# A two-layer decoder trunk on one core: new load order at the start, a reordered sequence of weight pairs, another attention pace, and a split last block

## The chip, the cores and the metric

The kernel runs on one NeuronCore of a Trainium2 chip. The metric is the device time of one execution in microseconds, the median of several runs. One execution of each kernel is also recorded by the hardware profiler; its trace is what the rows below come from.

## What is computed

One inference step of a trunk of two layers over 1024 prompt positions and 8 sample rows (1032 columns in the kernel's layout), width 1024, all in float32. The reference of a layer, shortened:

```
xa, za, u, v, zb, q, k, vv, zc, gates = split(x @ w_in)      # 5632 columns
ya = pool_mix(xa)                    # causal windows 2/4/8/16, mean minus x, 64x64 mix
yb = u * spatial(layer_norm(v))      # 128-position chunks, lower-triangular weights
yc = window_attention(rope(q), rope(k), vv, sinks)           # window 128, 8 heads, 2 kv heads
g  = sigmoid(gates + b_gate)         # 3 x 1024
merged = g0*((ya*silu(za)) @ w_pa) + g1*((yb*silu(zb)) @ w_pb) + g2*((yc*silu(zc)) @ w_pc)
x  = layer_norm(ALPHA*x + merged @ w_out)
```

Beside the two results the step returns the pooling state, the key and value caches and the normalised v rows.

## The kernel before

**Arithmetic.** Every float32 operand is split into a rounded part h and a remainder lo (`split`, L96: ACT writes h, VectorE writes lo), and a product is three matmuls, h by h, h by lo and lo by h. x lies transposed in XH and XL, 8 tiles of 128 rows by 1032 columns.

**Stages of a layer.** (1) `a0` (L348) computes v and the input of its norm for nine row blocks with the eight weight slices w0 (wA); block b needs x block b, split by `split_x`. Its normalisation (`a0_post`) reads the rows lrow. (2) `rope` (L382) makes keys and queries, with weights wB. (3) Eighteen *pairs* (`pair`, L870): each computes two column tiles of w_in with seven products of 24 matmuls (a Strassen scheme: `product`, quarters of x and sums of quarters T2, T3, T4), and evacuates partial sums with VectorE adds (L878) and a `use` function of the pair: `gates` (12 pairs: tanh on ACT into two tiles, stored to DRAM by ACT's queue), `pair_xa` (the input of the pooling), `pair_z` (two: silu2 of za, zb), `pair_u`, `gate_c` (two: silu of zc times the attention's output). (4) `project` (L980): 24 steps (branch i, tile d); a step multiplies a branch output by its weights, and VectorE (L1000) multiplies with the gate read back from DRAM. (5) the output projection `d_mm` in two column halves, then `d_ln`, `d_out`, for nine row blocks in the order 0, 1, 2, 8, 3, 4, 5, 6, 7.

**What sets the order.** It is written out by hand; each engine runs its instructions in program order. Small work is put between matmuls by `Jobs` (L29): each call of `pump` is a tick; a pair has 21 (two in each product, L866, and seven in `pair`). List 1 is the attention; a step of it that uses TensorE blocks the list for `pace` ticks (L343). `need(key)` runs whatever is still open up to that key. Weights come by `Feed` (L80): SP issues a load when a raw buffer (six tiles "wr") is free; `prep` splits one; four split weights ("wh") fit. GpSimd makes the weight sums that a pair needs (L210 to L219), and the sums of the pooling (L770, L775), which VectorE finishes (`pool_widen` L795, `pool_mean` L805); `pool_mix` (L818) follows on TensorE. Big tiles are named by slots (x0 to x11, u4 to u11): a tile waits until the slot's previous user is done. All DMAs share a small set of semaphores used in turn, so an issue also waits until an earlier DMA on its semaphore has landed.

**Loads at the start.** SP issues x0's first half, wA0, wA1, x0's second half, wA2 to wA5, x1; ACT issues x3, x5, x7 (L1103); SP goes on with wA6, wA7, ident, x2, lrow, x4, x6, the sample rows, lcol, cb, then six tiles of wB.

Of the kernel before, what the change touches and what calls it, by code (L numbers as in the profile page):

```python
# [8 lines left out]
F32 = mybir.dt.float32  # L9
F32R = mybir.dt.float32r  # L10
AF = mybir.ActivationFunctionType
ALU = mybir.AluOpType
# [4 lines left out]
L = 2  # L17
# [5 lines left out]
DM = 1024  # L23
SEGS = ((0, 384), (384, 384), (768, 264))
ALPHA = 4.0 ** 0.25
EPS = 1e-5


# [51 lines left out]
class Feed:  # L80
# [2 lines left out]
    def __init__(self, nc, new, items):  # L83
        self.nc, self.new, self.items, self.raw = nc, new, deque(items), deque()

    def stage(self, n=1):
        for _ in range(n):
            if self.items:
                src = self.items.popleft()
                c = src.free_size()  # L90
                t = self.new()[:, 0:c]
                self.nc.sync.dma_start(out=t, in_=src)
                self.raw.append(t)

# [7 lines left out]
def trunk_kernel(  # L102
# [23 lines left out]
    def t_acc():  # L126
        return acc.tile([128, 512], F32, tag="acc", name="acc")
# [16 lines left out]
    def t_sm(n, name, bufs=4):  # L144
        return sm.tile([128, n], F32, tag=name, name=name, bufs=bufs)

    def t_u(s, shape, dt=F32, name="u"):

        return big.tile([128] + shape, dt, tag=s, name=f"{name}{s}")
# [16 lines left out]
    def blk(b):  # L166
        return slice(b * 128, b * 128 + 128) if b < NB else slice(S, T)
# [4 lines left out]
    def order():  # L172
        for l in range(L):
            yield from [wA[l, :, k] for k in range(8)]
            yield from [wB[l, j, :, 4 * h:4 * h + 4] for j in range(5) for h in range(2)]
            yield from [wS[l, p, q] for p in range(18) for q in range(4)]
            yield from [wP[l, d, :, h * 512:h * 512 + 512] for h in range(2) for d in range(2)]
            for d in range(2, 8):
                yield from [wP[l, d, :, h * 512:h * 512 + 512] for h in range(2)]
                if d >= 4:  # L180
                    yield wO[l, 0, :, d - 4]
            yield from [wO[l, 0, :, k] for k in range(4, 8)]
            yield from [wO[l, 1, :, k] for k in range(8)]
# [12 lines left out]
    def prep(n=1):  # L196
        for _ in range(n):
            if todo:
                todo.popleft()()
# [45 lines left out]
    class Slices:  # L245
# [2 lines left out]
        def __init__(self, slots, cols=512):  # L248
            self.h, self.lo, self.slots, self.cols = {}, {}, slots, cols

        def prep(self, n=1):
            for _ in range(n):
                k, c = len(self.h), self.cols
                if k < 8:
                    if len(self.slots) == 4 and k == 0:
                        self.p = t_p(name="slp")
                    t = self.p[:, k] if len(self.slots) == 4 and k < 4 else t_u(self.slots[k % len(self.slots)], [T], F32R, "sl")
                    self.h[k], self.lo[k] = t[:, 0:c], t[:, 512:512 + c]
                    split(nc, self.h[k], self.lo[k], feed.raw.popleft())
                    feed.stage()  # L260

    ident = const.tile([128, 128], F32, name="ident")
    cb = const.tile([128, 428], F32, name="cb")
# [74 lines left out]
    class Layer:  # L338
        def __init__(self, l):
            self.l, self.c, self.jobs = l, LC[l], Jobs()  # L340
            self.s, self.pt, self.res, self.rr, self.row, self.y = [{} for _ in range(6)]
            self.late, self.step, self.out = deque(), 0, []
            self.jobs.pace = 2.8  # L343
            self.kT = t_u("u10", [T], F32, "kT")
            self.v = t_u("u11", [NB, 128], F32, "v")
            self.vs = lay.tile([NS, 128], F32, name="vs")
# [573 lines left out]
            out(0, 1)  # L920
            pump()

        def gates(self, i, d, extra={}):
            O = [t_u(s, [T], F32, "g") for s in (("u8", "u9") if d % 4 else ("u6", "u7"))]

            def use(c, q, s, p):
                o = O[c][:, q * HT + s * 258:q * HT + s * 258 + 258]
                A.activation(o, p, AF.Tanh, bias=self.c["h"][:, i * 8 + d + c:i * 8 + d + c + 1], scale=0.5)  # L928
                if s and (c, q) in ((1, 0), (0, 1)):
                    A.dma_start(out=gd[i][d + c], in_=O[c])  # L930

            self.pair(use, O, extra)

        def gate_c(self, j, extra={}):
            O = [t_u(s, [T], F32, "z") for s in (("u6", "u7") if j else ("u4", "u5"))]

            def use(c, q, s, p):
                e = slice(q * HT + s * 258, q * HT + s * 258 + 258)
                t, o, y = t_w2()[:, 0:258], O[c][:, e], self.ycr[:, j + c, e]
                A.activation(t, p, AF.Tanh, scale=0.5)  # L940
                V.scalar_tensor_tensor(o, t, 1.0, p, op0=ALU.add, op1=ALU.mult)
                V.scalar_tensor_tensor(y, o, 0.5, y, op0=ALU.mult, op1=ALU.mult)

            self.pair(use, O, extra)

        def split_y(self, j, eng=None):
            h, lo = [t_u(f"x{4 + 2 * j + i}", [T], F32R, "yh") for i in range(2)]
# [32 lines left out]
        def project(self):  # L980
            for x, (i, d) in enumerate(self.steps):
# [5 lines left out]
                for q in range(2):  # L987
# [21 lines left out]
                        self.late.append((self.step + 1, lambda d=d, q=q, m=m[:, e]: self.merged(d, q, m)))  # L1009
                    if (i < 2 and q) or (i == 2 and not q and d >= 3):  # L1010
                        prep()
                if x < 3:
                    self.split_c((1, 3, 2)[x])
                if x == 0:
                    for q in range(2):
                        self.load_gate(0, 1, q)
# [16 lines left out]
        def d_mm(self, b, h, w):  # L1033
            n = rows(b)
            x = self.res.pop((b, h))
            p = mm_rows(b, w, self.jobs)
            if h == 0:
                if b < NB:
                    t = t_u(("u11", "u10", "u4", "u5", "x0", "x1", "x2", "x3")[b], [T], F32, "rr")
                    self.row[b] = [t[:, 0:512], t[:, 512:1024]]  # L1040
                else:
                    self.row[b] = [whp.tile([128, 512], F32, tag="wh", name="rs") for _ in range(2)]
                self.rr[b] = t_sm(16, "rr", 9)
            r = self.row[b][h]
            V.scalar_tensor_tensor(r[:n], x[:n, 0:512], 2 * ALPHA, p[:n], op0=ALU.mult, op1=ALU.add)  # L1045
            V.bn_stats(self.rr[b][:n, h * 6:h * 6 + 6], r[:n])  # L1046

        def d_ln(self, b):
            n, c = rows(b), self.c
            rw = self.row[b]  # L1050
            st, mv = self.rr[b][:, 0:12], self.rr[b][:, 12:14]
            V.bn_aggr(mv[:n], st[:n])  # L1052
            rstd_of(mv, n, 4 * EPS)
            g, be = c["lng"], c["lnb"]
            if self.l == L - 1 and b == NB - 1:
                for h in range(2):
                    r = rw[h]
                    V.scalar_tensor_tensor(r, r, mv[:, 0:1], g[h], op0=ALU.subtract, op1=ALU.mult)  # L1058
                for h in range(2):
                    r = rw[h]  # L1060
                    V.scalar_tensor_tensor(r, r, mv[:, 1:2], be[h], op0=ALU.mult, op1=ALU.add)  # L1061
                return
            for h in range(2):
                r = rw[h][:n]
                V.tensor_scalar(r, r, mv[:n, 0:1], mv[:n, 1:2], op0=ALU.subtract, op1=ALU.mult)
            for h in range(2):
                r = rw[h][:n]
                V.tensor_tensor(r, r, g[h][:n], op=ALU.mult)
                G.tensor_tensor(r, r, be[h][:n], op=ALU.add)
# [29 lines left out]
    def load_x(b, ks=slice(0, 8)):  # L1099
        if b not in xraw:  # L1100
            t = t_u(f"x{b if b < 4 else b + 4}" if b < NB else "u8", [T], F32, "x")
            xraw[b] = t[:, 0:8 * rows(b)].rearrange("p (k t) -> p k t", k=8)
        (A if b in (3, 5, 7) else SP).dma_start(out=xraw[b][:, ks], in_=xb[b][:, ks] if b < NB else xs[:, ks])  # L1103

    def split_x(b, ks=slice(0, 8)):
        split(nc, XH[:, ks, blk(b)], XL[:, ks, blk(b)], xraw[b][:, ks])
        if b == NB:
            stack_sample()
# [6 lines left out]
    feed.stage(2)  # L1115
    load_x(0, hi_k)
    feed.stage(4)
    load_x(1, lo_k)
    load_x(1, hi_k)
    w0 = Slices(WA, 384)  # L1120
    split_x(0, lo_k)
    w0.prep(2)
    SP.dma_start(out=ident, in_=c_a)
    for b in range(2, NB + 1):
        load_x(b)
        if b == 2:
            load_rows(0)
    load_layer(0)
    SP.dma_start(out=cb, in_=c_b)
    V.memset(mhalf, -0.5)  # L1130
    V.memset(XS.bitcast(F32), 0.0)
    split_x(0, hi_k)
    w0.prep(6)

    order_d = [0, 1, 2, 8, 3, 4, 5, 6, 7]
    left = []
    for l in range(L):
# [35 lines left out]
                J.need(("TT", n, k))  # L1173
        y.t1_parts()
        y.queue_sample()
        for i in range(3):
            for d in range(0, 8, 2):
                if (i, d) == (0, 2):
                    J.need("sp")
                y.gates(i, d, {3: lambda: J.need(("T1", 3))} if (i, d) == (0, 0) else {})  # L1180
        J.need(("P", NB - 1, 1))
        y.pair_xa()
        y.ya = y.pair_z(("u8", "u9"))
        y.queue_mix()
        J.need(("pool", 1))
# [3 lines left out]
        y.pair_u()  # L1189
        J.need(("sgu", 1))  # L1190
        y.gate_c(0)
        y.open_gates()
        for i, d in ((0, 0), (1, 0)):
            for q in range(2):
                y.load_gate(i, d, q)
        y.gate_c(2, {2: lambda: y.split_y(0), 21: lambda: y.split_y(1), 3: lambda: y.split_y(2),
                     1: lambda: y.split_y(3), 4: lambda: y.split_c(0)})
        for q in range(2):
            y.load_gate(1, 1, q)
        cur["w0"] = w0 = Slices(WA)  # L1200
# [140 lines left out]
```

## Time and profile before

| | |
|---|---|
| median of 3 runs | 1469.99 us (1469.11 to 1471.54) |
| profiled execution | 1468.98 us, its span 1467.2 us |
| TensorE matmuls | 1436.6 us busy, 98% of the span |
| VectorE, ACT, GpSimd busy | 70%, 41%, 30% |
| mean granted TensorE clock | 0.999 |
| layer 0 | first blocks from 4.89 us, pairs 107.6 to 540.0, projection from 540.0 |
| last matmul starts, span ends | 1459.15, 1467.2 us |

How to read it: TensorE is busy almost throughout, so the profile is read for the moments in which it isn't: the waits of TensorE with the instruction that ended them. Windows give the busy time of each engine between two moments; here they are cut at the pair boundaries.

### The profile page before, as it was taken

The numbers are of one execution on the slowest core, as the hardware profiler recorded it, in microseconds if no ns is written. First come the engines' busy times: TensorE is split into PE (matmuls) and PEld (weight loads), VectorE is DVE, ScalarE is ACT, GpSimd is POOL, SyncE is SP. The second block draws the span as 40 slices with busy tenths as digits, with TensorE's granted clock in tenths as the row PEclk, the third lists the DMA queues.
The fourth block names the chain that finished last, engine by engine and source line by source line (L and its number), as shares of the span: only waits on it lengthen the run. The fifth ranks groups of instructions, "written<-read, shape, count | busy, mean of one in ns | idle before, by whom it ended". The sixth has DMA issues, their size and how long they took to land. (4 is left out here: it accounts for less than half of the span.)

```text
span 1467.2 us, 27711 instructions
## 1 busy us (share of the span) xinstructions
PE 1436.6 (98%) x10592; PEld 1356.2 (92%) x10592; DVE 1030.5 (70%) x2330; ACT 603.3 (41%) x1419; POOL 438.7 (30%) x434
## 2 busy tenths in 40 slices
PE   7999999999999999999999999999999999999997
PEld 7999999999998999988799999999999999999876
DVE  6997676676558687654889966666665777966547
ACT  4375565556533252220224745555565232422100
POOL 0114334141242205500530251423321522054015
PEclk9999999999999999999999999999999999999999
DMA  6312222323223135643324122222222231466413
GB/s 253 125 46 80 87 94 66 102 73 102 73 84 76 44 102 188 204 142 94 134 93 139 53 73 96 79 95 73 86 89 102 55 83 38 132 187 194 130 48 126
DMA packets 82388, 151.92 MB, mean 104 GB/s; under 512 B 13216, under 2 KB 22512, under 8 KB 82224
## 3 DMA queue, kind: packets, MB, share of 16 engines
q1 hardware_dynamic: 65184, 114.34, 25.6%
q10 hardware_dynamic: 17072, 35.81, 6.3%
q8 instruction: 83, 1.36, 0.4%
q14 instruction: 49, 0.40, 0.1%
HBM read 113.62 MB, written 38.58 MB: 104 GB/s over the span
## 5 line engine op out<-in xcount | busy, mean ns | idle before, releaser
L862 PE MATMUL acc<-XH,wh 128*128 128x258 f32 x1152 | 235.9, 286 | 2.0 <-DVE zyu L878 2.0
L862 PE MATMUL acc<-XH,wl 128*128 128x258 f32 x1152 | 236.1, 286 | 0.0
L862 PE MATMUL acc<-XL,wh 128*128 128x258 f32 x1152 | 235.2, 285 | 0.0
L98 DVE TENSOR_TENSOR wl<-wr,wh 128x512 fp32r<-128x512 f32 x196 | 161.1, 822 | 97.3 <-ACT wh L97 96.7
L862 PEld LDWEIGHTS acc<-XH,wh 128*128 128x128 f32 x1152 | 178.7, 189 | 7.2 <-issue 6.5
L862 PEld LDWEIGHTS acc<-XH,wl 128*128 128x128 f32 x1152 | 178.4, 189 | 5.5 <-issue 5.0
L862 PEld LDWEIGHTS acc<-XL,wh 128*128 128x128 f32 x1152 | 178.7, 189 | 4.7 <-issue 4.2
L97 ACT ACTIVATE wh<-wr 128x512 fp32r<-128x512 f32 x196 | 122.3, 624 | 116.3 <-PE acc L862 48.2
L211 POOL TENSOR_TENSOR st<-st,wr 128x512 f32<-128x512 f32 x36 | 49.5, 1376 | 312.0 <-DVE wl L98 230.7
L98 DVE TENSOR_TENSOR wl<-st,wh 128x512 fp32r<-128x512 f32 x108 | 76.9, 712 | 71.9 <-ACT wh L97 71.1
L1002 POOL TENSOR_TENSOR glu<-glu,glu 128x516 f32<-128x516 f32 x56 | 80.8, 1460 | 145.9 <-DVE glu L1000 117.1
L319 PE MATMUL acc<-slx,XH 128*128 128x512 f32 (+1 forms) x384 | 114.1, 379 | 0.4 <-DVE slx L98 0.4
L878 DVE TENSOR_TENSOR gu<-gu,acc 128x258 f32<-128x258 f32 x240 | 89.7, 414 | 29.5 <-PE acc L862 29.5
L928 ACT ACTIVATE gu<-gu,halves 128x258 f32<-128x258 f32 x144 | 65.6, 504 | 104.7 <-DVE gu L878 104.2
L862 PE MATMUL acc<-T2x,wh 128*128 128x258 f32 x576 | 98.1, 287 | 1.2 <-DVE yc L395 1.2
L862 PE MATMUL acc<-T3x,wh 128*128 128x258 f32 x576 | 96.2, 286 | 1.6 <-DVE gu L878 1.6
L486 ACT ACTIVATE ap<-ap,ns 128x256 f32<-128x256 f32 (+1 forms) x128 | 62.4, 489 | 83.7 <-DVE ns L484 82.9
L862 PE MATMUL acc<-T4x,wh 128*128 128x258 f32 x576 | 96.1, 285 | 0.0
L210 POOL TENSOR_TENSOR st<-wr 128x512 f32<-128x512 f32 x36 | 50.7, 1407 | 143.2 <-DVE wl L98 66.5
L218 POOL TENSOR_TENSOR st<-wr,st 128x512 f32<-128x512 f32 x36 | 50.1, 1391 | 121.7 <-issue 121.3
L862 PEld LDWEIGHTS acc<-T2x,wh 128*128 128x128 f32 x576 | 80.9, 189 | 3.5 <-DVE yc L395 1.4
L319 PEld LDWEIGHTS acc<-slx,XH 128*128 128x128 f32 x384 | 71.9, 191 | 11.7 <-DVE slx L98 0.9
(246 smaller groups left out, 3444.8 us busy)
## 6 DMA issues: line engine op xcount, KB each, us to landing
wr<-in_wS_dram SPq DMA_DIRECT2D x144, 256.0 KB
gd<-gu ACTq DMA_DIRECT2D x48, 516.0 KB
glu<-gd SPq DMA_DIRECT2D x96, 258.0 KB
wr<-in_wP_dram SPq DMA_DIRECT2D x32, 256.0 KB
wr<-in_wO_dram SPq DMA_DIRECT2D x32, 256.0 KB
wr<-in_wB_dram SPq DMA_DIRECT2D x20, 256.0 KB
w<-in_xp_dram SPq DMA_DIRECT2D x16, 256.0 KB
w<-x2d SPq DMA_DIRECT2D x16, 256.0 KB
```

What stands on the lines that cost most here:

```text
L97: nc.scalar.activation(h, raw, AF.Copy)
L98: (eng or nc.vector).tensor_tensor(lo, raw, h.bitcast(F32), op=ALU.subtract)
L210: G.tensor_tensor(s1[:, 0:512], a21, a22, op=ALU.add)
L211: G.tensor_tensor(s2[:, 0:512], s1[:, 0:512], a11, op=ALU.subtract)
L218: G.tensor_tensor(s4[:, 0:512], a12, sums[p][1], op=ALU.subtract)
L319: PE.matmul(p[:, 0:n], x[:, k, blk(b)], c, start=(i == 0 and j == 0), stop=(i == len(terms) - 1 and j == len(t) - 1))
L486: A.activation(o, o, AF.Exp, bias=nm[:, i:i + 1], scale=-1.0, accum_out=su[:, i:i + 1])
L862: PE.matmul(ps[s][:, 0:258], a[:, c], b[:, s * 258:s * 258 + 258], start=(first and k == 0 and j == 0), stop=(k == 3 and j == 2), skip_gro ...
L878: V.tensor_tensor(part(c, q, s), part(*a, s), b[s][:, 0:258], op=ALU.add)
L928: A.activation(o, p, AF.Tanh, bias=self.c["h"][:, i * 8 + d + c:i * 8 + d + c + 1], scale=0.5)
L1002: (V if last else G).tensor_tensor(m[:, e], m[:, e], t[:, e], op=ALU.add)
```

## The change

The loads of the first blocks are issued in another order: all eight wA slices come before x1 (two of them into "st" tiles), four wB tiles are issued ahead of x2, all x loads are issued by SP, ident and cb come later, and four wA slices are split before the second half of x0. The pace of the attention goes from 2.8 to 2.3 ticks. Ten gate pairs stand ahead of pair_xa where there were twelve; gate pair (2, 4) follows pair_xa, in tiles u8 and u9, and gate pair (2, 6) stands last, behind both gate_c pairs, in u6 and u7; the four split_y and two split_c are done in it, so two split_c instead of three are left to the projection. The order of the weights (PAIRS) follows. In the last layer the last block's second half is computed in two accumulators of 256 columns with their own statistics, and block 6 too is normalised in the fused form that block 7 had.

```diff
+PAIRS = (0, 1, 2, 3, 4, 5, 6, 7, 8, 9, 12, 10, 13, 14, 15, 16, 17, 11)
...
-            yield from [wS[l, p, q] for p in range(18) for q in range(4)]
+            yield from [wS[l, p, q] for p in PAIRS for q in range(4)]
...
-            self.jobs.pace = 2.8
+            self.jobs.pace = 2.3
...
-        def gates(self, i, d, extra={}):
-            O = [t_u(s, [T], F32, "g") for s in (("u8", "u9") if d % 4 else ("u6", "u7"))]
+        def gates(self, i, d, us, extra={}):
+            O = [t_u(s, [T], F32, "g") for s in us]
...
-            O = [t_u(s, [T], F32, "z") for s in (("u6", "u7") if j else ("u4", "u5"))]
+            O = [t_u(s, [T], F32, "z") for s in (("u4", "u5") if j else ("u6", "u7"))]
...
-                if x < 3:
-                    self.split_c((1, 3, 2)[x])
+                if x < 2:
+                    self.split_c((3, 2)[x])
...
+            last = self.l == L - 1 and b == NB - 1 and h
+            p = None if last else mm_rows(b, w, self.jobs)
...
+            if last:
+                for e in (slice(0, 256), slice(256, 512)):
+                    p, q = t_acc(), e.start // 256
+                    for k in range(8):
+                        for j, (a, c) in enumerate(((XH, w.h[k]), (XH, w.lo[k]), (XL, w.h[k]))):
+                            PE.matmul(p[:, 0:256], a[:, k, blk(b)], c[:, e], start=(k == 0 and j == 0), stop=(k == 7 and j == 2))
+                    V.scalar_tensor_tensor(r[:, e], x[:, e], 2 * ALPHA, p[:, 0:256], op0=ALU.mult, op1=ALU.add)
+                    V.bn_stats(self.rr[b][:, 12 + q * 6:18 + q * 6], r[:, e])
+                return
...
-            if self.l == L - 1 and b == NB - 1:
+            if self.l == L - 1 and NB - 2 <= b < NB:
...
-        (A if b in (3, 5, 7) else SP).dma_start(out=xraw[b][:, ks], in_=xb[b][:, ks] if b < NB else xs[:, ks])
+        SP.dma_start(out=xraw[b][:, ks], in_=xb[b][:, ks] if b < NB else xs[:, ks])
...
     feed.stage(4)
+    feed.stage(2, t_st)
     load_x(1, lo_k)
     load_x(1, hi_k)
     w0 = Slices(WA, 384)
     split_x(0, lo_k)
-    w0.prep(2)
-    SP.dma_start(out=ident, in_=c_a)
+    w0.prep(4)
     for b in range(2, NB + 1):
...
     load_layer(0)
+    SP.dma_start(out=ident, in_=c_a)
     SP.dma_start(out=cb, in_=c_b)
+    split_x(0, hi_k)
+    w0.prep(2)
+    w0.prep(2, 0)
...
-    split_x(0, hi_k)
-    w0.prep(6)
...
-        for i in range(3):
-            for d in range(0, 8, 2):
-                if (i, d) == (0, 2):
-                    J.need("sp")
-                y.gates(i, d, {3: lambda: J.need(("T1", 3))} if (i, d) == (0, 0) else {})
+        for i, d in [(i, d) for i in range(3) for d in range(0, 8, 2)][:10]:
+            if (i, d) == (0, 2):
+                J.need("sp")
+            y.gates(i, d, ("u8", "u9") if d % 4 else ("u6", "u7"),
+                    {3: lambda: J.need(("T1", 3))} if (i, d) == (0, 0) else {})
         J.need(("P", NB - 1, 1))
         y.pair_xa()
+        y.gates(2, 4, ("u8", "u9"))
         y.ya = y.pair_z(("u8", "u9"))
...
         y.gate_c(0)
+        y.gate_c(2)
         y.open_gates()
...
-        y.gate_c(2, {2: lambda: y.split_y(0), 21: lambda: y.split_y(1), 3: lambda: y.split_y(2),
-                     1: lambda: y.split_y(3), 4: lambda: y.split_c(0)})
+        y.gates(2, 6, ("u6", "u7"), {2: lambda: y.split_y(0), 21: lambda: y.split_y(1), 3: lambda: y.split_y(2),
+                                     1: lambda: y.split_y(3), 4: lambda: (y.split_c(0), y.split_c(1))})
```

## Rows read from the trace of the kernel before

**Rows 1.** Waits of TensorE: line waited for: us in total, times, longest.

```profile
PE acc L319 <- ACT slp L97: 7.6, 2, 4.9
PE att L995 <- ACT ychx L97: 3.1, 2, 1.5
...
PE acc L862 <- DVE zyu L878: 2.0, 2, 1.0
...
PE att L821 <- DVE xau L805: 1.2, 2, 0.6
...
PE att L995 <- DVE yclu L98: 1.1, 2, 0.6
PE att L821 <- DVE zyu L823: 1.0, 2, 0.5
PE att L995 <- DVE glu L1000: 1.0, 2, 0.5
```

**Rows 2.** Windows (us; PE, PEld, DVE, ACT, POOL busy): two gate pairs, pair_xa, z pair.

```profile
207.80:257.70 49.90, 49.90 (x411) 47.75 (x409) 33.71 (x94) 29.50 (x79) 17.91 (x24) 1.00 0.27 85
406.30:426.50 20.20, 20.20 (x170) 20.20 (x169) 9.45 (x18) 6.38 (x13) 3.84 (x3) 1.00 0.35 104
426.50:448.20 21.70, 20.71 (x171) 20.45 (x170) 19.06 (x27) 5.69 (x13) 17.56 (x15) 1.00 0.16 48
```

**Rows 3.** Timeline, start of layer 0's projection: start us, us, instruction, idle before.

```profile
539.97 0.65 PE L995 MATMUL att<-yhx,wh 128*128 128x258 f32 x4
...
545.50 0.43 DVE L942 SCALAR_TENSOR_TENSOR yc<-zu,yc 128x258 f32<-128x258 f32 x1
...
546.00 0.80 SPq L973 DMA_DIRECT2D glu<-gd  x2
...
552.64 0.63 ACT L97 ACTIVATE wh<-wr 128x512 fp32r<-128x512 f32 x1 [5.15 <-issue]
```

**Rows 4.** Timeline of the first blocks.

```profile
4.80 4.25 ACTq L1103 DMA_DIRECT2D xx<-in_xb_dram  x3
...
9.10 0.63 ACT L97 ACTIVATE XH<-xx 128x512 fp32r<-128x512 f32 x1 [3.78 <-DMA wr<-in_wA_dram]
...
14.67 0.84 PE L319 MATMUL acc<-slx,XH 128*128 128x384 f32 x2
...
16.80 1.05 ACT L97 ACTIVATE XH<-xx 128x1024 fp32r<-128x1024 f32 x1
...
17.83 1.56 PE L319 MATMUL acc<-slx,XH 128*128 128x384 f32 x8
...
18.90 1.22 DVE L98 TENSOR_TENSOR XL<-xx,XH 128x1024 fp32r<-128x1024 f32 x1
...
20.64 0.50 PE L319 MATMUL acc<-slp,XH 128*128 128x384 f32 x2
```

**Rows 5.** Windows of the start; the last two columns are DMA share and GB/s.

```profile
0.00:12.00 12.00, 4.27 (x10) 3.06 (x11) 4.26 (x10) 5.21 (x9) 0.20 (x4) 1.00 0.81 278
12.00:16.00 4.00, 4.00 (x14) 3.76 (x13) 1.62 (x4) 1.81 (x4) 0.00 (x0) 1.00 1.04 413
```

**Rows 6.** Timeline of TensorE, end of layer 0's attention.

```profile
398.47 1.08 PE L519 MATMUL att<-ap,vu 128*64 128x256 f32 x8
```

**Rows 7.** Timeline of VectorE in the pooling.

```profile
436.92 1.71 DVE L795 SCALAR_TENSOR_TENSOR pxyu<-pxyu,cb 128x512 f32<-128x512 f32 x1
...
452.83 0.75 DVE L795 SCALAR_TENSOR_TENSOR pxyu<-pxyu,cb 128x512 f32<-128x512 f32 x1
```

**Rows 8.** Chain that ended last: start us, us, what.

```profile
1431.78 27.77 PE acc L319 x120
```

**Rows 9.** Timeline of VectorE: statistics of 256 columns, and the kernel's end.

```profile
17.00 0.42 DVE L358 BATCH_NORM_STATS2 sv<-acc 128x6 f32<-128x256 f32 x1
...
1459.58 0.69 DVE L1045 SCALAR_TENSOR_TENSOR rrx<-w,acc 128x512 f32<-128x512 f32 x1 [0.49 <-PE acc L319]
1460.30 0.69 DVE L1046 BATCH_NORM_STATS2 rr<-rrx 128x6 f32<-128x512 f32 x1
```

More of the change, by code (lines that the diff above doesn't have):

```diff
@@ L84, in __init__, with stage @@
         self.nc, self.new, self.items, self.raw = nc, new, deque(items), deque()
-    def stage(self, n=1):
+    def stage(self, n=1, new=None):
         for _ in range(n):
@@ L90, in stage @@
                 c = src.free_size()
-                t = self.new()[:, 0:c]
+                t = (new or self.new)()[:, 0:c]
                 self.nc.sync.dma_start(out=t, in_=src)
@@ L249, in __init__, with prep @@
             self.h, self.lo, self.slots, self.cols = {}, {}, slots, cols
-        def prep(self, n=1):
+        def prep(self, n=1, stage=1):
             for _ in range(n):
@@ L259, in prep @@
                     split(nc, self.h[k], self.lo[k], feed.raw.popleft())
-                    feed.stage()
+                    feed.stage(stage)
     ident = const.tile([128, 128], F32, name="ident")
@@ L932, in gates, with gate_c @@
             self.pair(use, O, extra)
-        def gate_c(self, j, extra={}):
-            O = [t_u(s, [T], F32, "z") for s in (("u6", "u7") if j else ("u4", "u5"))]
+        def gate_c(self, j):
+            O = [t_u(s, [T], F32, "z") for s in (("u4", "u5") if j else ("u6", "u7"))]
             def use(c, q, s, p):
@@ L942, in use @@
                 V.scalar_tensor_tensor(y, o, 0.5, y, op0=ALU.mult, op1=ALU.mult)
-            self.pair(use, O, extra)
+            self.pair(use, O)
         def split_y(self, j, eng=None):
@@ L1035, in d_mm @@
             x = self.res.pop((b, h))
-            p = mm_rows(b, w, self.jobs)
+            last = self.l == L - 1 and b == NB - 1 and h
+            p = None if last else mm_rows(b, w, self.jobs)
             if h == 0:
@@ L1042, in d_mm @@
                     self.row[b] = [whp.tile([128, 512], F32, tag="wh", name="rs") for _ in range(2)]
-                self.rr[b] = t_sm(16, "rr", 9)
+                self.rr[b] = t_sm(26, "rr", 9)
             r = self.row[b][h]
+            if last:
[7 more added lines that the diff above has]
+                return
             V.scalar_tensor_tensor(r[:n], x[:n, 0:512], 2 * ALPHA, p[:n], op0=ALU.mult, op1=ALU.add)
+            if self.l == L - 1 and b == NB - 1:
+                for q in range(2):
+                    V.bn_stats(self.rr[b][:, q * 6:q * 6 + 6], r[:, q * 256:q * 256 + 256])
+                return
             V.bn_stats(self.rr[b][:n, h * 6:h * 6 + 6], r[:n])
@@ L1050, in d_ln @@
             rw = self.row[b]
-            st, mv = self.rr[b][:, 0:12], self.rr[b][:, 12:14]
+            st, mv = self.rr[b][:, 0:24 if self.l == L - 1 and b == NB - 1 else 12], self.rr[b][:, 24:26]
             V.bn_aggr(mv[:n], st[:n])
```

## The prediction

> **What bounds the kernel now.** I read the waits of TensorE first, then windows cut at the pair boundaries, then the timelines around each place where TensorE stood. TensorE is the bound nearly everywhere: a pair with no other work in it runs its 168 matmuls in 20.2 us, 0.120 us each [rows 2], and nothing on another engine shortens that. So only the time in which TensorE stands can be won, and the list is short [rows 1]: 7.6 us on the first block's weight slices, and, once in each layer, three waits around the pooling branch (zyu L878, xau L805, zyu L823: 1.0 + 0.6 + 0.5 = 2.1 us) and three at the start of the projection (glu, ychx, yclu: 0.5 + 1.55 + 0.55 = 2.6 us). The reader is to see that the totals come in twos. Idle time is counted from the modelled end of a matmul: four matmuls show 0.65 us, so one is taken as 0.29 long [rows 3], though the next could start after 0.12. Each wait thus cost about 0.17 more than is shown: 2.6 us a layer at the pooling and 3.1 at the projection. After the last matmul comes a short chain on VectorE.
>
> **Change, part 1: the load order.** ACT issues three x loads at 4.80 and is held in that for 4.25 us; its next split, of the second half of x0, starts only at 9.10 [rows 4]. TensorE stood 2.7 us for what follows on it (7.6 less the first 4.9 [rows 1]). With those loads on SP, ACT goes on as soon as wA2 is there; I let 2.5 of the 2.7 go (bounds 0 and 2.7). The granted clock reads 1.00 here [rows 5], yet two matmuls of 384 columns take 0.84 us at 14.67, 0.32 apart, which is the 1.2 GHz level; eight start 0.176 apart at 17.83 (1.56 in all), the 2.4 GHz level [rows 4]. If block 0 still runs wholly at the lower level, as it did, block 1 starts at 17.83 - 8 x 0.176 - 2.5 = 13.9 and ends 24 x 0.176 = 4.2 later, at 18.1. Then block 2 needs x2, and before that VectorE must finish block 0's normalisation, which needs lrow. SP is now passed by everything: x0, wA, x1 and four wB tiles (0.52 + 1.57 + 0.52 + 1.05 MB) stand ahead of x2 (0.52) and lrow (0.27), 4.46 MB to the end of lrow. The DMA engines move 278 GB/s over the first 12 us, 413 after that [rows 5]: 12 + (4.46 - 3.34)/0.413 = 14.7. From the last byte to the waiting instruction I add at most 1.3: before, 4.78 MB stood up to the end of x2, 15.5 by the same rates, and its split began at 16.80 [rows 4]. So lrow serves at 16.0, two VectorE steps of about 0.48 follow, then the split of x2 (1.22 [rows 4]), 18.2; block 2's third matmul waits for that, so by the loads block 2 counts from 17.85, by TensorE from 18.1. It began at 20.64 [rows 4]: 2.8 or 2.5 us are gained, and I take 2.6. Bounds: 4.5 if loads land faster than this and the clock rises early; a loss of 0.5 if x2 is held behind the wB tiles, which must wait for their buffers. Moving ident, cb and the memsets back costs nothing: their users (attention, the sample rows) come blocks later.
>
> **Part 2: the attention's pace, 2.8 to 2.3.** There are 80 paced TensorE steps in a layer and 21 ticks in a pair (two in each of seven products, seven between them). The first step stands in the last tick of pair 1, the last at 398.47 [rows 6], two thirds through pair 12 (tick 245): 224 ticks for 79 steps of 2.8 and a start-up of 3. At 2.3 it takes 182 and some 4, and ends near tick 207; ten gate pairs have 210. So the work fits, barely, and the flush by need(("P", 7, 1)) finds nothing. TensorE's own work is the same, only denser. VectorE: two gate pairs with attention take 33.71 us of 49.90, one pair without 9.45 [rows 2], so attention costs it 7.4 us a pair, now 7.4 x 2.8/2.3 = 9.0; the pair grows by the same denser TensorE work from 24.95 to 26.0, and VectorE's share from 68 to 71%. I cost this at 0.5 us over both layers; bounds 0 and 4 (0.2 a pair).
>
> **Part 3: a gate pair between pooling input and pooling gate.** After pair_xa, GpSimd adds up the windows and VectorE finishes them; before, this fell on the z pair, where VectorE was busy 19.06 of 21.70 us [rows 2] and TensorE stood for it. While GpSimd works, VectorE's own steps stretch: the same 128x512 L795 took 1.71 us at 436.92 and 0.75 at 452.83 [rows 7]. In the gate pair the eight silu steps of VectorE (0.37 to 0.43 each, 3 us) are missing, since tanh there is ACT's, so two of them (0.7 us) no longer stand before the late L878: of the 1.2 us that it cost, 0.4 stays. The second half of the pooling falls in the z pair that follows, with GpSimd nearly free, and the mix finds its input ready: its two waits go. 2.6 - 0.4 = 2.2 a layer, 4.4 in all; bounds 5.2 and 0. A wait is added: the z pair writes u8/u9, which the gate pair's last store must have left. The store is issued some 1.7 us after the pair's end, 0.53 MB take 1.3 at 0.413, and 1.3 to be seen: 4.3. The first write to that tile follows the second product, 5.8 us in. It is hidden with 1.5 us to spare; without that cover VectorE, and TensorE behind it, would stand by the difference.
> The Trainium skill, SBUF — State Buffer, section "Who interferes with whom", says that a VectorE instruction with two SBUF inputs and a GpSimd instruction that reads SBUF exclude each other for the whole instruction. The stretched L795 agrees. By that rule the splits and pooling steps are held in the gate pair just as in the z pair; that is the first rival below.
>
> **Part 4: last pair and start of the projection.** Both gate_c pairs now end a pair earlier, and the last is gates(2, 6). Before, the projection started at 539.97 with VectorE still in gate_c(2)'s tail until 545.9 (545.50, 0.43 [rows 3]); three split_c followed, and the third stood behind a weight split that ACT could start only at 552.64 [rows 3], 5 us late. After, VectorE's tail is two adds (0.75), two split_c remain, and both are issued before that weight split. VectorE then needs per step four L1000, a weight split and a split_c, some 3.4 us (4 x 0.37, 0.7, 1.2) against 24 x 0.12 = 2.9 of TensorE, twice, which four PSUM pairs cover. I leave 0.35 of the 3.1: 2.75 a layer, 5.5 in all. Bounds: 6.2 and a loss of 1.5. Added wait: load_gate(1, 1) reads into u6, which now must have been stored (two splits of 1.05 [rows 4] and the tanh stand before it on ACT: about +2.5; landed +5.1, an estimate by the same 1.3 and 1.3); behind it in SP's queue stand the loads of gate (0, 1) and a weight tile. SP issued (1, 1) at 546.00, +6.0, before [rows 3], so it isn't later than it was.
>
> **Part 5: the tail.** Last block: 48 matmuls of 256 columns at 0.121 (5.81) for 24 of 512 at 27.77/120 = 0.231 (5.55) [rows 2, 8]: +0.26. VectorE's step after it goes from 0.69 to 0.43, bn_stats from 0.69 to 0.42 [rows 3, 9], the aggregate of 24 values +0.06: 0.2 gained. Block 6 in four fused steps (2.8 us) starts a microsecond sooner since the first two don't wait for GpSimd, so it is off VectorE when block 7's second half arrives; if it weren't, 0.5 is lost. Bounds: 0.8 gained, 0.3 lost.
> By the Trainium skill, TensorE: Matmul & The Clock Gate, section "Back-to-back issue gap" (N/2.4 + 2.5 ns for a matmul by itself), the halves would cost 0.06 in place of 0.26; the rows decide.
>
> **Sum.** 2.6 + 4.4 + 5.5 + 0.2 - 0.5 = 12.2. The profiled execution took 1468.98 (span 1467.2 and 1.8 around it), so 1456.8; the median of the runs is 1.0 above it, and 1457.8 is the forecast.
>
> **Rivals.** (A) GpSimd holds VectorE in the gate pair as it did in the z pair, so that part 3 wins only the mix waits: 1.2 a layer instead of 2.2, or none if the backlog is carried on: 1459.8 to 1462.2. For it: the stretched rows; against: 3 us less for VectorE in that pair. 0.13. (B) The projection's gate loads come late behind the store of u6, and TensorE waits for PSUM as it did for the splits: part 4 is gone, 1463.3. For it: the new wait stands at the head of SP's queue; against: (0, 1) is needed by TensorE only when its step's PSUM comes round again, four steps of 24 matmuls in, at +11.6, and lands by about +9. 0.10. (C) x2 behind the wB tiles eats part 1: 1460.4. 0.07. (D) Slower: the denser attention makes VectorE late in the gate pairs. The price is that of the z pair, 1.4 a pair (21.70 against 20.2 [rows 2]) in 20 pairs, 28 us: 1457.8 + 28 = 1486. It decides where VectorE's share nears that pair's 88%; the mean comes to 71%. 0.03.
>
> **How the numbers follow.** The forecast has 0.67, with its own range 1454.5 to 1460.5. The best bounds together give 1453.3; A to C reach 1463.3, and the cheap end of D and the worst bounds lie beyond: 1453.3 to 1464. A difference of 0.2% (2.9 us) is what a measurement of this kernel can tell from none: below 1467.0 is faster. Forecast and A to C all lie there, with something off for two of them together: faster 0.91, within 0.05, slower 0.04.
>
> **What would show it.** Part 1: the second half of x0 split near 8 us, and block 2 starting near 17.9. Part 2: the last L519 in the tenth pair, gate pairs of 26 us, and no new TensorE wait on L878 in them. Part 3: no waits at L821 and under 0.5 at L862 in the pair after pair_xa. Part 4: no wait on ychx. Part 5: last matmul to end shorter by 0.5. Wrong would be a wait of TensorE on VectorE in most gate pairs, or L995 waiting on gate loads.

## The result and the profile after

The changed kernel takes 1507.21 us (median of 5 runs, 1505.23 to 1511.87) against 1471.54 (1469.11 to 1472.21) in the same comparison: ratio 1.0256, 95% interval 1.0244 to 1.0267. It is slower by 2.6%, outside the predicted range and on the side that had 0.04. The profiled execution took 1506.05 us with a span of 1504.3: 37.1 more than before. By stage, in us, from TensorE's first matmul of one to the first of the next, the first stage from the span's start (the last column is a mended version that comes below):

| stage | before | after | mended |
|---|---|---|---|
| first blocks, rope | 107.58 | 106.12 | 105.56 |
| layer 0: 18 pairs | 432.39 | 449.99 | 429.27 |
| layer 0: projection, output, next rope | 295.79 | 296.09 | 294.23 |
| layer 1: 18 pairs | 430.74 | 448.74 | 427.56 |
| layer 1: projection to the end of the span | 200.7 | 203.4 | 199.2 |

The pairs lost 35.6 us. Waits of TensorE in the kernel after, as in [rows 1]: line waited for, us in total, times, longest.

```profile
PE acc L863 <- DVE gu L879: 12.5, 16, 1.7
PE att L996 <- DVE glu L1001: 6.6, 2, 4.0
PE acc L320 <- ACT slp L98: 5.4, 2, 4.9
PE acc L863 <- DVE zyu L879: 4.3, 2, 2.2
PE acc L863 <- ACT gu L889: 3.5, 6, 1.3
PE att L509 <- DVE ap L499: 3.1, 6, 0.7
...
PE att L479 <- DVE ksu L457: 1.8, 2, 0.9
```

The wait for the add of a gate pair (gu) was small before; its line, which [rows 1] leaves out, is:

```profile
PE acc L862 <- DVE gu L878: 1.6, 2, 0.8
```

Here sixteen such waits head the list, with the attention's own steps (ap, ksu) further down. The two waits at the pooling's mix (L821) and those for ychx and yclu are gone, as predicted, but zyu has grown from 2.0 to 4.3 and glu from 1.0 to 6.6. Windows of the kernel after, columns as in [rows 2] with the DMA share and GB/s last: the start (as [rows 5]), two gate pairs with attention (pairs 4 and 5 counted from 0), a stretch in the first of them, gate pair (2, 4), z(ya), which is the pair that computes za.

```profile
0.00:12.00 12.00, 6.49 (x17) 5.28 (x18) 5.47 (x12) 7.08 (x13) 0.20 (x4) 1.00 0.81 272
12.00:16.00 4.00, 4.00 (x20) 4.00 (x19) 2.02 (x6) 0.56 (x3) 0.41 (x1) 1.00 0.85 315
...
212.46:268.17 55.71, 53.73 (x420) 50.87 (x421) 38.31 (x106) 32.34 (x88) 14.90 (x16) 0.97 0.24 79
...
218.70:222.10 3.40, 3.40 (x18) 3.40 (x17) 2.01 (x6) 2.80 (x7) 0.00 (x0) 0.50 0.77 242
...
400.45:422.17 21.72, 20.72 (x170) 20.39 (x169) 18.21 (x23) 5.98 (x13) 17.47 (x15) 1.00 0.15 46
422.17:445.87 23.70, 21.31 (x169) 20.61 (x169) 17.66 (x38) 9.05 (x20) 5.84 (x5) 1.00 0.39 96
```

Two gate pairs take 55.71 us where the prediction had 2 x 26.0, and VectorE's share of them is 38.31/55.71 = 69%, about the 68% of [rows 2]. It isn't saturated. Where it stands is seen in the timeline of one stall, all engines, layer 0 (start us, us, instruction; in brackets the idle time before it and what ended that):

```profile
210.39 1.28 POOL L211 TENSOR_TENSOR st<-wr 128x512 f32<-128x512 f32 x1
...
210.56 1.51 DVE L499 TENSOR_SCALAR ap<-ap,ns 128x256 f32<-128x256 f32 x2
...
212.00 0.74 DVE L879 TENSOR_TENSOR gu<-gu,acc 128x258 f32<-128x258 f32 x2
212.44 0.91 ACT L929 ACTIVATE gu<-gu,halves 128x258 f32<-128x258 f32 x2 [2.69 <-DVE gu L879]
...
213.76 0.42 ACT L456 ACTIVATE ksu<-yc 64x256 fp32r<-64x256 f32 x1 [0.40 <-ACT gu L929]
...
214.21 0.42 DVE L457 SCALAR_TENSOR_TENSOR ksu<-yc,ksu 64x256 fp32r<-64x256 f32 x1 [1.47 <-ACT ksu L456]
...
215.19 0.51 ACT L487 ACTIVATE ap<-ap,ns 128x256 f32<-128x256 f32 x1 [1.01 <-DVE ns L485]
...
216.28 0.61 ACT L98 ACTIVATE wh<-wr 128x512 fp32r<-128x512 f32 x1
216.93 0.69 DVE L99 TENSOR_TENSOR wl<-wr,wh 128x512 fp32r<-128x512 f32 x1 [1.17 <-ACT wh L98]
217.53 0.75 DVE L879 TENSOR_TENSOR gu<-gu,acc 128x258 f32<-128x258 f32 x2
...
218.01 1.07 PE L863 MATMUL acc<-T2x,wh 128*128 128x258 f32 x4 [1.73 <-DVE gu L879]
```

Read it from the bottom. TensorE waits for the last add of the pair before, whose products ended at 212.46. The add starts at 217.53 because of what is ahead of it in VectorE's queue: there stands the remainder of a weight split (L99), which waits for ACT's half; that stands in ACT's queue behind the attention's exponentials, these wait for VectorE's L485, which stands behind L457, and that waits for ACT's L456, behind the tanh of the evacuation before. The two engines hand each other the work and both idle: VectorE 1.47 and 1.17 us of these five. GpSimd adds to it at the start: the two L499 take 1.51 us beside L211, and 0.61 where GpSimd is idle (the same step at 210.30 in the run with the chain cut, below). I call this the hand-over chain.

### The profile page after: what moved, and what is told of

Its sections match the earlier page's. It is cut to its first block, busy times and chain, and to the rows that moved or that the text cites. A ratio compares the mean times of both kernels' runs of the same rounds, so it can differ in the third digit from the quotient of the medians.

```text
span 1504.3 us, 27743 instructions
## 1 busy us (share of the span) xinstructions
PE 1453.3 (97%) x10616; PEld 1365.1 (91%) x10616; DVE 1055.0 (70%) x2333; ACT 600.2 (40%) x1419; POOL 434.2 (29%) x432
## 4 chain that ended last, share of the span: by engine, by line
PE 39%; DVE 13%; ACT 5%; issue 4%; DMA 1%; POOL 1%; ACTq 0%; DVEq 0%; SPq 0%; POOLq 0%
PE acc L863 13%; PE acc L320 10%; PE att L996 6%; PE acc L996 5%; DVE wl L99 3%; PE acc L621 2%; ACT gu L929 1%; ACT wh L98 1%; ACT ap L487 1%; DVE ap L499 1%; DVE gu L879 1%; PE acc L327 1%; DVE ap L485 1%; DVE ksu L457 1%; DVE XL L99 0%
## 5 line engine op out<-in xcount | busy, mean ns | idle before, releaser
L863 PE MATMUL acc<-XH,wh 128*128 128x258 f32 x1152 | 239.5, 288 | 8.7 <-DVE gu L879 4.4
L99 DVE TENSOR_TENSOR wl<-wr,wh 128x512 fp32r<-128x512 f32 x196 | 156.8, 800 | 92.1 <-ACT wh L98 91.5
L99 DVE TENSOR_TENSOR wl<-st,wh 128x512 fp32r<-128x512 f32 x108 | 77.0, 713 | 80.0 <-ACT wh L98 77.9
L879 DVE TENSOR_TENSOR gu<-gu,acc 128x258 f32<-128x258 f32 x240 | 89.9, 416 | 11.0 <-PE acc L863 10.8
L211 POOL TENSOR_TENSOR st<-wr 128x512 f32<-128x512 f32 x36 | 50.5, 1402 | 152.3 <-DVE wl L99 100.9
L863 PEld LDWEIGHTS acc<-T3x,wh 128*128 128x128 f32 x576 | 81.8, 192 | 9.3 <-DVE zyu L879 4.7
```

The source lines that it names most:

```text
L99: (eng or nc.vector).tensor_tensor(lo, raw, h.bitcast(F32), op=ALU.subtract)
L211: G.tensor_tensor(s1[:, 0:512], a21, a22, op=ALU.add)
L863: PE.matmul(ps[s][:, 0:258], a[:, c], b[:, s * 258:s * 258 + 258], start=(first and k == 0 and j == 0), stop=(k == 3 and j == 2), skip_gro ...
L879: V.tensor_tensor(part(c, q, s), part(*a, s), b[s][:, 0:258], op=ALU.add)
```

## The experiments

**Pace or order?** The kernel before with one number changed:

```diff
-            self.jobs.pace = 2.8
+            self.jobs.pace = 2.3
```

> The kernel before with one number changed: pace 2.3 for 2.8; order, loads and tail as before. Theory 1 (the denser attention alone makes TensorE wait for the adds of the pairs): the gate pairs that hold attention lose as in the changed kernel, 15.8 us in layer 0 and some 15 in layer 1, so about 1470 + 31 = 1501 us. Theory 2 (the new order and its tiles are the cause, the pace is harmless): within 3 us of 1470.

Measured: 1501.39 us (1500.55 to 1503.49), ratio 1.0213 [1.0196, 1.0231]. The pace alone costs 31.5 us, nearly all of the loss, and its waits are those of after: gu L878 9.3 us in 12 waits. The listed waits don't add up to the loss; where the rest lies is told at the run with the chain cut.

**Is it the density?** The kernel after with pace 2.1.

> The changed kernel with pace 2.1 for 2.3. A pair has 21 ticks: at 2.8 the attention's steps fall on the same places in every second pair (15 steps in 42 ticks, three rounds of five), at 2.1 in every pair (10 in 21, two rounds of five), at 2.3 they drift through all places. Theory 1a (density: more steps in a pair, more waiting): slower than the changed kernel, 1507 + 5 to 15 us. Theory 1b (place: what costs is that a step falls between an add and the next one, and 2.3 meets every place): it goes either way by more than 10 us, and all gate pairs of a layer come out alike, within 0.5 us of each other.

Measured: 1474.28 (1471.36 to 1478.09), ratio 1.0027 [1.0015, 1.0039]. Denser, and 33 us faster, so the density by itself is not the cause. In layer 0 the fourth to the ninth gate pair come out alike, 26.26 to 26.31 us each, as theory 1b has it; the first three (27.05, 24.88, 25.67) and the last (21.45, in which the attention ends) don't. That the place of the steps is what counts is tested below.

**Without the attention.** Both orders with the attention over the prompt left out (it is not queued, so its output is missing):

```diff
-            if j == 0:
-                y.queue_att()
...
-        J.need(("P", NB - 1, 1))
```

> The kernel before without the prompt's attention steps (scores, softmax, transposes, values are left out; the rest stands). TensorE's work in them is about 44 us a layer, so about 1470 - 88 - 13 (their waits and switches) = 1370 us. It is the base for the next one.

> The changed kernel without the same attention steps. Theory 1 (the attention's pace is the loss): against the kernel before without attention it differs only by start, pooling, projection and tail, which the two traces put at -1.5, +1.75 x 2, +0.3 to +2.7 and -0.3: between 0 and +5 us. Theory 2 (order): +30 us.

Measured: 1372.43 for before, 1382.41 for after. Without any attention the rest of the change costs 10.0 us, by two runs of each. That is more than the 0 to 5 expected here, and the prediction had a gain of 12.7 (the sum without part 2). In the second kernel TensorE waits 9.9 us for the gate steps of the projection (glu) and 4.7 for adds of gate pairs, in the first 0.9 for glu and none of those adds. So two losses are to be explained: the attention in the gate pairs, and the places to which gate pairs were moved.

**Start and tail alone**, with the old order and pace 2.8.

> The kernel before with two parts of the change alone: the new load order and the split last block; order of the pairs and pace 2.8 stay. Theory 1 (these parts do what the trace of after shows there): pair 0 starts 1.5 us earlier (106.1 for 107.6) and the tail is some 0.3 shorter, so 1.8 us less than before: ratio 0.9988. The prediction's terms (2.6 + 0.2) would give 0.9981. Rival: the earlier start is given back in the pairs, ratio 1.000.

Measured: 1469.37, ratio 0.9995 [0.9986, 1.0004]: no difference that can be told, and the expected 0.9988 lies inside. These parts are not the loss.

**The hand-over chain cut.** The kernel after at its pace of 2.3. In the pairs VectorE's half of a weight split is kept back and issued behind the next evacuation (and the load of the freed buffer behind it); nothing else is changed:

```diff
-        split(nc, h[:, 0:n], lo[:, 0:n], raw)
+        A.activation(h[:, 0:n], raw, AF.Copy)
+
+        def low():
+            V.tensor_tensor(lo[:, 0:n], raw, h[:, 0:n].bitcast(F32), op=ALU.subtract)
+            feed.stage(stage)
+
+        lows.append(low)
         ready.append((h, lo))
-        feed.stage(stage)
...
             self.product(2, B_, True)
             add(0, 1, (1, 0), B_)
+            flush()
```

> The kernel after at its pace of 2.3, with one thing moved: in the pairs VectorE's half of a weight split (the remainder) is issued behind the evacuation of the product in which ACT's half was issued, instead of right behind ACT's half. No work is added or left out. Theory 1 (in the gate pairs TensorE waits for a VectorE add that is queued behind steps that wait for ACT, and the remainder behind ACT's half is the last of them): the gate pairs lose at least half of their 2 to 4 us of standing, so 15 us or more over both layers, 1507 goes to 1492 or below. Rival (VectorE is held by GpSimd's use of the memory, or is simply too busy in this density): the same work waits as long, 1504 to 1510.

Measured: 1470.59 (1468.74 to 1474.53), 36.6 less than after, ratio to before 1.0003 [0.9992, 1.0013]. Its waits of TensorE, then the same two gate pairs, and the same place in the pair on VectorE and ACT:

```profile
PE att L1017 <- DVE glu L1022: 7.8, 2, 4.2
PE acc L332 <- ACT slp L98: 5.3, 2, 4.7
PE att L521 <- DVE ap L511: 3.0, 4, 0.9
...
PE acc L875 <- ACT zyu L902: 1.9, 2, 1.0
```

```profile
206.88:258.21 51.33, 51.33 (x422) 49.12 (x421) 37.64 (x108) 31.04 (x86) 13.89 (x16) 1.00 0.26 83
```

```profile
208.04 0.75 DVE L891 TENSOR_TENSOR gu<-gu,acc 128x258 f32<-128x258 f32 x2
...
208.65 0.61 ACT L193 ACTIVATE wh<-wr 128x512 fp32r<-128x512 f32 x1
...
209.30 0.69 DVE L196 TENSOR_TENSOR wl<-wr,wh 128x512 fp32r<-128x512 f32 x1 [0.51 <-ACT wh L193]
```

No wait for a gu add is left; the last add of the pair before starts 1.2 us into the next pair, not 5.1, and the remainder follows it. Two pairs take 51.33 for 55.71 with the same work. The rival, that VectorE is held by GpSimd or too busy, is out as the main cause: VectorE's busy time is nearly the same and GpSimd's sums are all still there. The windows of the ten gate pairs of layer 0 show that the waits listed for TensorE are only half of the price: 274.09 us become 257.91, of which 8.2 is counted as idle time of TensorE (10.8 to 2.6), while the other 8.0 is counted as busy (263.29 to 255.27) with the same matmuls. A wait is counted only from the modelled end of a matmul, and the matmuls right behind one still follow each other late (the four at 272.64, behind a listed wait of 0.93 us, take 0.96 us, four at 426.71 without a wait 0.64); for 3.4 us the clock was lower too (last section).

**The place of a step at one density.** Pace 2.1 with the whole attention one tick later (`(("K", 1), 4)` to 5), and then the same with the chain cut.

> The kernel after with pace 2.1 (as in the run that gave 1474.3), and the whole attention one tick later: its steps of a layer then stand at other places of the same pairs, in the same number and density. Theory 1 (the place of a step within the pair decides): the gate pairs change from their 26.3 us by more than 0.5 us each, 10 us or more over 20 pairs, to either side. Rival (only the drift of 2.3 from pair to pair is bad; a pattern that repeats in each pair is good anywhere): within 3 us of 1474.3.

> Pace 2.1 and the attention one tick later, which gave 1484.7 where 1474.3 stood without the tick, and with VectorE's halves of the weight splits behind the evacuation. Theory 1 (the place of a step matters only because the halves stand in the way of the adds): the tick costs nothing any more, 1468 to 1473, like the 1470.6 at pace 2.3. Rival (the place costs by something else too): 1476 or more.

Measured: 1484.69 (1483.51 to 1488.86), 10.4 more than without the tick, and with the chain cut 1466.18 (1465.08 to 1467.74). In the run without the tick, with it, and with tick and cut, the ten gate pairs of layer 0 take 256.85, 261.25 and 255.71 us. So the tick costs 4.4 us there, and 4.1 in layer 1, a little less than theory 1 expected; the rest lies in z(ya), 2.1 us more in layer 0, where the clock also read 0.50 for 3.4 us, and behind it. Windows of two gate pairs, of the one with the tick and then of the one with tick and cut:

```profile
210.77:264.34 53.57, 53.34 (x435) 50.60 (x433) 36.17 (x114) 32.74 (x93) 17.53 (x24) 1.00 0.25 80
```

```profile
208.44:261.10 52.66, 52.66 (x435) 49.99 (x434) 42.27 (x116) 33.23 (x92) 17.98 (x24) 1.00 0.26 81
```

One tick moves the time by more than the forecast's own range was wide (6.0 us). With the chain cut TensorE is busy throughout these two pairs, though VectorE is then at 42.27/52.66 = 80%. Pace 2.1 with the cut and without the tick was not run.

**The gate loads of the projection.** The kernel after at pace 2.1, with the loads that wait for the last gate pair's store put behind those that don't:

```diff
-        for q in range(2):
-            y.load_gate(1, 1, q)
...
                         self.load_gate(0, 1, q)
+                    for q in range(2):
+                        self.load_gate(1, 1, q)
```

> The kernel after with pace 2.1, and the loads of gate (1, 1), which wait for the last gate pair's store, issued behind the loads of gate (0, 1) instead of ahead of them. Theory 1 (TensorE stands 3 to 4 us in the projection because the loads of (0, 1) wait behind that store on SP): the wait of L995 on the VectorE step with the gate goes, 3 us or more a layer, 1474.3 goes to 1468 or below. Rival (the VectorE queue is late there by itself, two remainders that wait for ACT stand ahead of the last add): the wait stays, 1473 to 1475.

Measured: 1469.23 (1467.82 to 1472.48), 5.1 less than 1474.28. TensorE's wait for glu falls from 7.5 to 3.1 us over both layers, and doesn't go: half of the theory. The other half is VectorE, whose split_c(2) (2.32 us beside GpSimd's gate sums, 1.23 for the split_c before it) stands ahead of the gate steps; the rival has a part.

**The store behind which z(ya) waits.** The chain cut, and the pooling's state stores of 60-byte elements moved from ACT's queue beside gate pair (2, 4) to behind the second z pair:

```diff
-            A.dma_start(out=sps_o[l, :, j], in_=self.st[:, j, :, 1:16])
...
+        for j in range(2):
+            A.dma_start(out=sps_o[l, :, j], in_=y.st[:, j, :, 1:16])
         y.pair_u()
```

> The kernel of the run that gave 1470.6 (after, VectorE's halves later), with one more thing moved: the two stores of the pooling's state (elements of 60 bytes), which ACT issues between the two stores of gate pair (2, 4) or behind them, come behind the second z pair. Theory 1 (the small store delays the second store of (2, 4) on the DMA queue, and z(ya) waits for that): z(ya) no longer waits for the store, 1.7 us of layer 0 and 2.0 of layer 1 go, 1470.6 goes to 1467. Rival (the store of 0.53 MB takes so long by itself, or ACT issues it too late): z(ya) stands as before, 1470 to 1471.

Measured: 1468.30 (1465.43 to 1469.65), 2.3 less than 1470.59. The pair takes 20.54 us in layer 0 and 20.25 in layer 1 instead of 21.99 and 22.34. VectorE still waits for the store, but starts 8.2 us into the pair instead of 9.6, which is enough for TensorE. The two pairs win 3.5 us together; TensorE's wait for glu grows at the same time, from 7.8 to 8.5. VectorE in z(ya) of this kernel:

```profile
412.55 0.76 DVE L890 TENSOR_TENSOR zyu<-zyu,acc 128x258 f32<-128x258 f32 x2 [1.72 <-DMA gd<-gu]
```

The add starts 4.5 us after its store was issued; in the run without this move it was 5.9, in the kernel after 6.9. The small store accounts for a part of the delay; the size of that part by itself was not measured.

**Is the cut a gain for any kernel?** The kernel before, with its own order, start and pace, and the chain cut.

> The kernel before, at pace 2.8 and with its own order and start, with VectorE's half of a weight split issued behind the evacuation. Theory 1 (the hand-over costs only where the steps of the attention fall badly, and in the kernel before they fall well: its gate pairs stand 0.4 to 0.8 us each): what can go are those and a part of the waits in the z pair, 0 to 4 us: ratio 0.997 to 1.000. Rival (the later halves are worth as much in any kernel, 37 us as in the kernel after): 0.975.

Measured: 1468.96 (1468.10 to 1470.58), ratio 0.9990 [0.9981, 0.9999]. There is little to win: at the pace of 2.8 TensorE's idle time in the trace of before is nil from the third gate pair to the twelfth, so its steps happen to stand where the chain doesn't close. What the cut wins in the first ten gate pairs (2.4 us in layer 0) it gives back in part at the pooling's mix, where TensorE's wait for xau goes from 1.2 to 4.0 us over both layers.

**All mended.** The kernel after at pace 2.3 with the chain cut, the loads swapped, the small stores later, and VectorE's halves of split_c(0) and split_c(1) behind the last add of pair (2, 6):

```diff
-                                     1: lambda: y.split_y(3), 4: lambda: (y.split_c(0), y.split_c(1))})
+                                     1: lambda: y.split_y(3), 4: lambda: (y.split_c(0, later), y.split_c(1, later))})
...
+        for run in later:
+            run()
```

> The kernel after at its pace of 2.3 with four things moved and none left out: VectorE's half of a weight split behind the evacuation (as in the run that gave 1470.6); the loads of gate (1, 1) behind those of gate (0, 1); VectorE's halves of split_c(0) and split_c(1) behind the last add of gate pair (2, 6); the pooling's small state store moved from ACT's queue in pair (2, 4) to behind the second z pair. Theory 1 (the order of the pairs is worth what the prediction said once these four places are out of its way): the two waits of L995 on the gate step, 7.8 us, and z(ya)'s standing of 1.7 and 2.0 go, so 1470.6 goes to 1458 to 1463, faster than before by 0.5 to 0.8%. Rival (VectorE's and ACT's work in the projection and behind the pooling is late by its amount, not by its order): 1466 or more.

Measured: 1458.50 us (1457.51 to 1460.08), ratio 0.9920 [0.9906, 0.9933]: 11.5 faster than before, 48.7 faster than after, and it beats both. Its longest waits of TensorE; gu and zyu are no longer found:

```profile
PE acc L332 <- ACT slp L98: 5.4, 2, 4.9
PE att L1020 <- DVE glu L1025: 3.1, 2, 1.5
PE att L521 <- DVE ap L511: 3.0, 4, 0.9
```

## Why the prediction was wrong, step by step

**Part 2 is the step that failed.** "I cost this at 0.5 us over both layers; bounds 0 and 4" stands against 31.5 measured with the pace alone. The work was counted rightly: the last attention product falls in the tenth gate pair (375.26), and VectorE's share stayed at 69%. What was wrong is the measure. The prediction asked whether VectorE has time, by its share over a pair, and not what stands ahead of each add in its queue. Rival (D) named the consequence and nearly its price, 1486, but tied it to a share of 88%; after loses at 69% and the kernels with the chain cut lose nothing in the two pairs shown at 73% (37.64/51.33) and 80%. So (D) isn't borne out as it was put. The answer lay in the order of the queues, which the timeline of before shows for its own pace only: at 2.8 a step's place repeats every two pairs (21 x 2 = 15 x 2.8), at 2.1 every pair, and at 2.3 it drifts, so that the ten pairs of layer 0 are from 0.0 to 3.9 us longer than the same pairs with the chain cut. These lengths are read from the traces; which combinations of ticks close the chain was not worked out.

The Trainium skill, PSUM — Partial Sum Buffer, section "Engine vs sequencer instructions", says that the queues of ScalarE, VectorE and GpSimd are strictly first in, first out. The stall above agrees: an add whose products had ended 5.1 us before waited behind a remainder.

**Part 3: the term of the added wait was mis-sized.** "The store is issued some 1.7 us after the pair's end" and seen after 4.3; the second product's add, the first write to the tile, ran at +11.3, behind a store that was issued at +4.4. VectorE and ACT in z(ya), layer 0 (the pair before ended at 422.17):

```profile
424.59 0.69 DVE L99 TENSOR_TENSOR wl<-wr,wh 128x512 fp32r<-128x512 f32 x1 [0.96 <-ACT wh L98]
425.20 0.75 DVE L879 TENSOR_TENSOR gu<-gu,acc 128x258 f32<-128x258 f32 x2
...
426.59 0.34 ACTq L931 DMA_DIRECT2D gd<-gu  x1
...
433.52 0.76 DVE L879 TENSOR_TENSOR zyu<-zyu,acc 128x258 f32<-128x258 f32 x2 [1.88 <-DMA gd<-gu]
```

The first delay is the hand-over chain again: the add, and behind it tanh and store, stand behind a remainder. So the store was to be 1.5 us early for a write at +5.8, and the write came 5.5 us late. Rival (A), GpSimd stretching VectorE in the gate pair, shows too: (2, 4) takes 21.72 for 20.2, with one idle time of TensorE of 1.0 us, while L805 on 16 columns took 1.20 us at 415.55 and 0.17 at 429.78. With the chain cut that idle time is gone (20.31) although GpSimd is busy for 16.19 us there, 17.47 before: the stretching by itself costs TensorE nothing. Mended, gate pair (2, 4) and both z pairs take 2.9 us less than pair_xa and both z pairs before (64.45 for 67.37, layer 0; a pair without other work takes 20.24 in both), more than the 2.2 predicted.

**Part 4: rival (B), at 0.10, happened for a part.** The prediction has the store "about +2.5", and of the loads of (1, 1) behind it, "so it isn't later than it was". Start of layer 0's projection (556.10) in the kernel after, VectorE, the queues and TensorE, as in [rows 3]:

```profile
557.58 2.38 DVE L99 TENSOR_TENSOR yclu<-yc,ychx 128x1032 fp32r<-128x1032 f32 x2 [2.12 <-ACT ychx L98]
...
560.48 0.75 DVE L879 TENSOR_TENSOR gu<-gu,acc 128x258 f32<-128x258 f32 x2
...
561.87 0.33 ACTq L931 DMA_DIRECT2D gd<-gu  x1
...
564.82 1.11 SPq L974 DMA_DIRECT2D glu<-gd  x2
...
566.51 2.74 SPq L974 DMA_DIRECT2D glu<-gd  x4
...
567.68 2.33 DVE L99 TENSOR_TENSOR yclu<-yc,ychx 128x1032 fp32r<-128x1032 f32 x1
...
570.96 0.76 DVE L1001 SCALAR_TENSOR_TENSOR glu<-glu,att 128x258 f32<-128x258 f32 x2 [0.96 <-issue]
571.53 0.63 PE L996 MATMUL att<-ychx,wh 128*128 128x258 f32 x2 [2.60 <-DVE glu L1001]
```

Two split_c stand ahead of the last adds, and VectorE stands 2.12 us until ACT has done its half; so tanh, store (+5.8), the loads of (1, 1) (+8.7) and behind them those of (0, 1) (+10.4) are all late, and TensorE stands 2.6 us here and 4.0 in layer 1. The run with the loads swapped puts a little over half of that down to them, the rest to the split_c at 567.68. The step that failed is "VectorE's tail is two adds (0.75)": what was put in front of these adds was left out. Mended, 1.5 us of standing is left in each layer, so in layer 0 part 4 gives 1.6 of its 2.75.

**Part 1: right in its working, 1.1 us off in one arrival.** Block 1 starts at 14.16 and block 2 at 18.34, 2.3 earlier than before. lrow serves VectorE at 17.11, not 16.0: 315 GB/s were moved from 12 to 16 us for the 413 of [rows 5], and with the windows of after the prediction's own sum gives 12 + (4.46 - 3.26)/0.315 + 1.3 = 17.1. x2's split then ends at 19.3, and block 2's third matmul, which waits for it, starts at 19.38 for 20.98, only 1.6 earlier. 1.46 of 2.6 reach the pairs.

```profile
14.16 1.56 PE L320 MATMUL acc<-slp,XH 128*128 128x384 f32 x8
...
17.11 0.48 DVE L363 SCALAR_TENSOR_TENSOR w<-acc,sv,lrow 128x256 f32<-128x256 f32 x1 [1.60 <-DMA lrow<-in_lrow_dram]
...
18.10 1.22 DVE L99 TENSOR_TENSOR XL<-xx,XH 128x1024 fp32r<-128x1024 f32 x1
18.34 0.51 PE L320 MATMUL acc<-slp,XH 128*128 128x384 f32 x2
...
19.38 0.44 PE L320 MATMUL acc<-slp,XL 128*128 128x384 f32 x1 [0.52 <-DVE XL L99]
```

**Part 5: right.** From the last matmul's start to the end of the span 8.05 us became 7.44 (1496.86 to 1504.3). From the first matmul of the last half block it is 13.4 and 13.0, so some 0.4 are gained where 0.2 was forecast: the 48 halves follow each other after 0.118 us and cost 0.13 more than the 24 whole ones, not 0.26. The last step on VectorE and its statistics are those predicted:

```profile
1497.18 0.42 DVE L1053 SCALAR_TENSOR_TENSOR rrx<-w,acc 128x256 f32<-128x256 f32 x1
1497.63 0.43 DVE L1054 BATCH_NORM_STATS2 rr<-rrx 128x6 f32<-128x256 f32 x1
```

**The sum.** 12.2 less was forecast, 1457.8; the mended kernel shows 1458.5. That the two lie so close is in part luck, for it is another kernel, and by the stages above its gains are others: 2.0 at the start for 2.6, 6.3 in the pairs for 3.9 (4.4 less 0.5), 3.1 behind them for 5.7 (parts 4 and 5). What the order was to give can be had; but parts 2, 3 and 4 depended on adds that had to come out of VectorE's queue in time, and none of these adds was followed through it.

## What to carry to other kernels

An engine with a third of its time free can still be late: before small work is packed denser or moved, write down what stands ahead of each evacuation in its engine's queue, and for each of those whom it waits for. Put the half of a two-engine step that must wait for the other engine behind the evacuation, not ahead of it; with that done, neither the pace of 2.3 nor that of 2.1 with the tick lost in the gate pairs what it had lost. A load that waits for a late store goes behind those that don't.

## What the runs showed of the hardware that was not expected

In some stalls of TensorE, or right behind them, the granted clock fell, so that they cost more than their length. In the kernel after, behind the stall of 1.73 us that ended at 218.01, the clock reads 0.50, the lower of its two levels, from 218.7 to 222.1: 18 matmuls in those 3.4 us, where a stretch at 1.00 (224.0 to 227.0) holds 28 in 3.0. By these rows that is some 1.5 us more, an estimate. The same happened in layer 1 behind the stalls of 2.2 us in z(ya) and 4.0 us at the projection. It doesn't follow from the length of the stall alone: behind the 2.1 us of z(ya) and the 2.6 us at the projection in layer 0, and behind 1.74 us at 960.8, the clock stayed at 1.00; in the run with the pace alone it also fell at 872.7, where no wait of TensorE is listed in the 10 us before. In the two runs with the attention left out, the new order shows 0.50 for 6.8 us from within each of its stalls of 5.0 us at the projection, the old order, which stands only 1.6 there, 1.00; and in the mended kernel the clock reads 1.00 up to its last matmul. The kernel with the chain cut alone shows 0.50 for 6.8 us from within its stall of 3.6 us there and for 3.4 us behind that of 4.2 us, so a part of what the mended one wins on it at the projection is the clock's.
